# Masked softmax: GpSimd shares ScalarE's fetch of the lengths, fills later, and opens its narrow loads one batch later

## The chip, the cores and the metric

The kernel runs on one core of a Trainium2 chip. The time is the device time of one execution, in microseconds (us). A core has TensorE (PE), VectorE (DVE), ScalarE (ACT), GpSimd (POOL) and SyncE (SP), each with its own queue of instructions; 16 DMA engines move data between main memory and the on-chip memory (SBUF), for all queues together. Engines wait for each other and for transfers by semaphores.

## What is computed

`x` is 16 batches x 8 heads x 256 x 256 in float32, `lengths` has one number from 128 to 255 for each batch. Each row is a softmax over its first `length` columns; the others are zero.

```python
for b in range(batch):
    length = lengths[b]
    masked = x[b, :, :, :length].copy()
    masked = masked - np.max(masked, axis=-1, keepdims=True)
    exp_masked = np.exp(masked)
    result[b, :, :, :length] = exp_masked / np.sum(exp_masked, axis=-1, keepdims=True)
```

## The kernel before

**Tiles.** A batch is 2048 rows of 256 columns: 128 partitions x 16 rows x 256, 2 MB. The tile `xt` has 8 slots of one batch each; batch b lives in slot b mod 8 from its load to its store, and every step works in place. The first four batches (`ahead = 4`) are loaded whole by SyncE's queue. The twelve others are loaded by GpSimd's queue, each only as wide as its length needs (`widths` 160 to 240 in steps of 8, or all 256). Since a narrow load doesn't fill the columns behind it, GpSimd first sets columns 160 to 255 of slots 4 to 7 to zero (L151, "the fills"), and the mask overwrites what is out of range in any case.

**SyncE (L107 to L123)** issues batch 0 in two halves (semaphores `s_ld[0]` and `s_ld[1]`), batches 1 to 3 (`s_ld[2]` to `s_ld[4]`, so batch b has `s_ld[b + 1]`), and then the stores of all batches in order. A store is cut into parts (`parts`, L50): a half and two quarters up to batch 9, two halves for batches 10, 11 and 15, one piece for 12 to 14. It waits for VectorE's divide of that part (`s_out`) and, from batch 2 on, until the store of batch b - 2 has landed. Whole loads and stores go through the same queue, q1 in the profile; GpSimd's loads are q0.

**GpSimd (L142 to L162)** writes the column numbers (`iota_i`) and `ones`, fetches the lengths for itself (`word_p`, L146), seeds the store semaphores, waits for VectorE's first step (`s_v` 1, the column bounds `down`), makes the four fills, and waits for its lengths, the fills, and `s_ld[ahead - 1]`: the landing of batch 2 (L152 to L154). Then a loop issues the narrow loads. It reads the batch's length into a register (L158), and from its third load on waits until the load two before has landed and the store that frees its slot has too (L160, L161); so two narrow loads at most are under way. `pick` (L127) branches to the load of the right width (L131).

**VectorE** makes `down` from `iota_i` (L180), casts the lengths that ScalarE's queue fetched (`word`, L110) to bf16 (L185), and from a TensorE product that spreads them over the partitions (L167) makes `len_s` (L188), the bounds by batch. Both L180 and L188 raise `s_v`. Then for every batch: `mask`, one clip of the batch (L197; batch 0 in halves), and `divide`, twice a reciprocal (L221) and a product of half a batch (L224). The order is written out: batch b + 1 is masked before batch b is divided (L233 to L240), so a batch that lands late holds up the divide, and the store, of the batch before it.

**ScalarE** issues the fetch of `word`, and then for every half batch takes eight exponentials with their row sums (L251), as soon as VectorE has clipped it.

Of the kernel before, what the change touches and what calls it, by code (L numbers as in the profile page):

```python
# [11 lines left out]
I32 = mybir.dt.int32  # L12
# [4 lines left out]
POOL = mybir.EngineType.Pool  # L17
# [3 lines left out]
def kernel(  # L21
# [6 lines left out]
    nc = tc.nc  # L28
    P = nc.NUM_PARTITIONS

    batch, heads, seq_q, seq_k = x.shape
# [10 lines left out]
    ahead = 4  # L42
# [18 lines left out]
    pool = ctx.enter_context(tc.tile_pool(name="all", bufs=1))  # L61
    psum = ctx.enter_context(tc.tile_pool(name="psum", bufs=1, space=bass.MemoryType.PSUM))
    xt = pool.tile([P, slots, nt, seq_k], F32, name="xt")
    word64 = pool.tile([1, batch], mybir.dt.int64, name="word64")
    word = word64.bitcast(I32)
    word64_p = pool.tile([1, batch], mybir.dt.int64, name="word64_p")
    word_p = word64_p.bitcast(I32)
    len_b = pool.tile([1, batch], BF16, name="len_b")
    ones = pool.tile([1, P], BF16, name="ones")
    len_f = psum.tile([P, batch], F32, name="len_f")  # L70
# [8 lines left out]
    with tc.tile_critical(no_gpsimd_drain=True):  # L79
        sem = lambda n: ctx.enter_context(nc.semaphore(n))  # L80
        s_word = sem("s_word")
        s_word_p = sem("s_word_p")
        s_ones = sem("s_ones")
        s_lenb = sem("s_lenb")
        s_lenf = sem("s_lenf")
        s_ld = [sem(f"s_ld{k}") for k in range(ahead + 1)]
# [6 lines left out]
        s_v = sem("s_v")  # L93
# [4 lines left out]
        def length(engine, at):  # L98

            return nc.values_load(  # L100
                at,
                engines=[engine],
                skip_runtime_bounds_check_because="compared with constants, never an address",
            )


        for h in range(2):  # L107
            s = slice(h * half, (h + 1) * half)
            nc.sync.dma_start(out=xt[:, 0, s], in_=x_f[0, :, s]).then_inc(s_ld[h], 16)  # L109
        nc.scalar.dma_start(out=word64, in_=lengths[None, :]).then_inc(s_word, 16)  # L110
        for b in range(1, ahead):
            nc.sync.dma_start(out=xt[:, b], in_=x_f[b]).then_inc(s_ld[b + 1], 16)  # L112
        for b in range(batch):
            s_b = s_st[b % 2]
            for s in parts(b):
                nc.sync.wait_ge(s_out, 2 * b + (s.stop - 1) // half + 1)
                if b >= 2 and s.start == 0:
                    nc.sync.wait_ge(s_b, 64 * (b // 2 + 1))
                nc.sync.dma_start(  # L119
                    out=out_f[b, :, s, :], in_=xt[:, b % slots, s, :]  # L120
# [6 lines left out]
        def pick(v, n, slot, par, ws):  # L127

            if len(ws) == 1:
                w = ws[0]  # L130
                nc.gpsimd.dma_start(  # L131
                    out=xt[:, slot, :, :w], in_=x_n[:, n, :, :w]
                ).then_inc(s_sw[par], 16)
                return
            m = (len(ws) - 1) // 2
            with nc.gpsimd.If(v <= ws[m]):  # L136
                pick(v, n, slot, par, ws[: m + 1])
            with nc.gpsimd.Else():  # L138
                pick(v, n, slot, par, ws[m + 1 :])
# [3 lines left out]
            iota_i, pattern=[[1, seq_k]], base=0, channel_multiplier=0  # L143
        ).then_inc(s_iota, 1)
        nc.gpsimd.memset(ones, 1.0).then_inc(s_ones, 1)  # L145
        nc.gpsimd.dma_start(out=word64_p, in_=lengths[None, :]).then_inc(s_word_p, 16)  # L146
        for par in range(2):
            nc.gpsimd.memset(seed[:, par : par + 1], 0.0).then_inc(s_st[par], 64)  # L148
        nc.gpsimd.wait_ge(s_v, 1)
        for b in range(ahead, slots):  # L150
            nc.gpsimd.memset(xt[:, b, :, low:], 0.0).then_inc(s_fill, 1)  # L151
        nc.gpsimd.wait_ge(s_word_p, 16)  # L152
        nc.gpsimd.wait_ge(s_fill, slots - ahead)
        nc.gpsimd.wait_ge(s_ld[ahead - 1], 16)  # L154
        with nc.Fori(0, (batch - ahead) // 2, 1, engines=[POOL]) as q:  # L155
            for par in range(2):
                n = 2 * q + (ahead + par)
                v_len = length(POOL, word_p[0:1, bass.ds(2 * n, 1)])  # L158
                with nc.gpsimd.If(q >= 1):  # L159
                    nc.gpsimd.wait_ge(s_sw[par], 16 * q)  # L160
                    nc.gpsimd.wait_ge(s_st[par], 64 * q)  # L161
                pick(v_len, bass.ds(n, 1), bass.ds(n % slots, 1), par, widths + [seq_k])  # L162
# [9 lines left out]
        def step(ins):  # L172
# [8 lines left out]
                out=down, in0=iota_i, scalar1=0.5, scalar2=-big, op0=ALU.add, op1=ALU.mult  # L181
# [7 lines left out]
                out=len_s, in0=len_f, scalar1=big, scalar2=None, op0=ALU.mult  # L189
# [56 lines left out]
        with nc.Fori(0, 2 * batch, 1, engines=[ACT]) as i:  # L246
            nc.scalar.wait_ge(s_min, i + 1)
            at = bass.ds(i % (2 * slots), 1)
            for j in range(half):
                e = x_h[:, at, j, :]  # L250
                ins = nc.scalar.activation(  # L251
                    out=e, in_=e, func=EXP, accum_out=sum_h[:, bass.ds(i, 1), j]
# [32 lines left out]
```

The softmax here doesn't subtract the row's maximum and nothing guards it: scores larger than these inputs give would overflow.

## Time and profile before

| | us |
|---|---|
| median of 14 runs (156.74 to 157.53) | 156.96 |
| the profiled execution | 156.46 |
| its span | 154.7 |
| VectorE busy | 120.4 |
| ScalarE busy | 105.1 |
| GpSimd busy | 19.4 |
| batch 0's halves landed | 6.2 and 8.7 |
| batches 1, 2 and 3 landed | 13.6, 18.5 and 24.1 |
| clip of batch 0's first half starts | 9.30 |
| first store issued | 16.73 |
| first narrow load issued | 20.69 |
| last store issued | 143.8 |

Times in the trace count from the span's start. In a row of the timeline the first number is when an instruction started and the second how long it took; what stands in brackets is the engine's idle time before it and what ended it. "Busy" of the DMA engines is the mean share of time in which a packet was under way on the 16 engines; it can be a little over 1 where packets overlap. A landing is the time at which a transfer's semaphore was complete.

### The profile page before, as it was taken

What the parts mean: (1) busy time and instruction counts of PE and PEld (TensorE: products, weight loads), DVE (VectorE), ACT (ScalarE), POOL (GpSimd) and SP (SyncE); (2) the same over time, 40 slices, a digit from 0 to 9 for tenths busy, and PEclk for the clock granted to TensorE, in tenths of its full rate; (3) what the DMA queues carried; (4) which work ended last, traced back from release to release, by engine and by line L of the source; (5) the groups of instructions that cost most, each with busy time, mean ns of one, the idle gap of its engine ahead of it and who ended that gap; (6) DMA issues with size and microseconds to landing.
All of it is one profiled execution on the core that took longest, in us unless ns stands there. A gap on an engine that the chain in (4) does not pass through costs nothing.

```text
span 154.7 us, 1320 instructions
## 1 busy us (share of the span) xinstructions
PE 0.2 (0%) x1; PEld 0.1 (0%) x1; DVE 120.4 (78%) x84; ACT 105.1 (68%) x514; POOL 19.4 (13%) x26
## 2 busy tenths in 40 slices
PE   0000000000000000000000000000000000000000
PEld 0000000000000000000000000000000000000000
DVE  4963999999999994939989499999894999970000
ACT  3019599999989694882959579889796597900000
POOL 7900031003030202002020021120100000000000
DMA  4999999999999999999999999999999999999993
GB/s 117 426 441 428 441 318 380 418 439 434 399 402 396 416 413 410 424 405 410 414 410 421 406 418 408 412 409 409 424 410 450 417 413 424 449 432 441 413 422 140
DMA packets 10452, 62.08 MB, mean 401 GB/s; under 512 B 930, under 2 KB 1026, under 8 KB 7122
## 3 DMA queue, kind: packets, MB, share of 16 engines
q1 hardware_dynamic: 6336, 41.95, 66.3%
q0 software_dynamic: 4112, 20.12, 32.1%
q14 instruction: 2, 0.02, 0.0%
q10 hardware_dynamic: 2, 0.00, 0.0%
HBM read 28.51 MB, written 33.55 MB: 401 GB/s over the span
## 4 chain that ended last, share of the span: by engine, by line
DMA 67%; DVE 15%; issue 3%; SPq 2%; POOLq 1%; DVEq 0%
DMA xt<-in_x_dram 38%; DMA out_dram<-xt 29%; DVE xt L224 10%; DVE xt L197 5%; SPq L119 2%; DVE inv_sum L221 1%; SPq L109 1%; POOLq L100 0%; POOLq L131 0%; POOLq L136 0%; SPq L112 0%; DVEq L214 0%; POOLq L155 0%; POOLq L159 0%; POOLq L138 0%
## 5 line engine op out<-in xcount | busy, mean ns | idle before, releaser
L251 ACT ACTIVATE xt<-xt x256 | 102.4, 401 | 28.6 <-DVE xt L197 28.6
L224 DVE TENSOR_TENSOR xt<-xt,inv_sum 128x2048 f32<-128x2048 f32 x32 | 73.3, 2292 | 1.1
L251 ACT ACTIVATION_READ_ACCUMULATOR xt<-xt x256 | 47.9, 187 | 0.0
L197 DVE SCALAR_TENSOR_TENSOR xt<-down,len_s,xt 128x2048 f32<-128x2048 f32 (+1 forms) x17 | 37.7, 2224 | 12.2 <-DMA xt<-in_x_dram 11.2
L131 POOL DMA_DIRECT2D xt<-in_x_dram x12 | 12.7, 1058 | 90.8 <-DMA out_dram<-xt 51.1
L221 DVE RECIPROCAL inv_sum<-row_sum 128x8 f32<-128x8 f32 x32 | 6.3, 195 | 2.4 <-ACT xt L251 2.4
L185 DVE CAST len_b<-word 1x16 bf16<-1x16 int32 x1 | 5.6, 5602 | 0.4 <-DMA word<-in_lengths_dram 0.4
L151 POOL MEMSET xt<- 128x1536 f32 x4 | 5.3, 1394 | 0.0
L243 ACT ACT_TABLE_LOAD x1 | 1.3, 1283 | 1.6 <-SPq L79 1.6
L180 DVE TENSOR_SCALAR down<-iota_i 128x256 f32<-128x256 int32 x1 | 0.3, 294 | 1.6 <-POOL iota_i L142 1.6
L146 POOL DMA_DIRECT2D word_p<-in_lengths_dram x1 | 0.6, 646 | 0.1
L188 DVE TENSOR_SCALAR len_s<-len_f 128x16 f32<-128x16 f32 x1 | 0.2, 175 | 0.3 <-PE len_f L167 0.3
L142 POOL IOTA iota_i<- 128x256 int32 x1 | 0.3, 332 | 0.6 <-SPq L79 0.6
L243 ACT ACTIVATE warm<-const-float32-0.0 128x1 f32<-128x1 f32 x1 | 0.2, 202 | 0.0
L145 POOL MEMSET ones<- 1x128 bf16 x1 | 0.2, 194 | 0.0
L167 PE MATMUL len_f<-len_b,ones 1*128 1x16 bf16 x1 | 0.2, 164 | 8.1 <-DVE len_b L185 8.1
L269 POOL MEMSET const-float32-0.0<- 128x1 f32 x1 | 0.1, 99 | 0.3 <-issue 0.3
L148 POOL MEMSET seed<- 1x1 f32 x2 | 0.1, 88 | 0.0
L167 PEld LDWEIGHTS len_f<-len_b,ones 1*128 1x128 bf16 x1 | 0.1, 99 | 8.0 <-issue 8.0
L269 POOL MEMSET const-float32-1.0<- 128x1 f32 x1 | 0.1, 99 | 0.0
L269 POOL MEMSET const-bfloat16-1.0<- 128x1 bf16 x1 | 0.1, 99 | 0.0
L269 POOL MEMSET const-uint8-127<- 128x1 uint8 x1 | 0.1, 99 | 0.0
(1 smaller groups left out, 0.0 us busy)
## 6 DMA issues: line engine op xcount, KB each, us to landing
out_dram<-xt SPq DMA_DIRECT2D x16, 1024.0 KB
out_dram<-xt SPq DMA_DIRECT2D x20, 512.0 KB
xt<-in_x_dram SPq DMA_DIRECT2D x3, 2048.0 KB, 16.0
out_dram<-xt SPq DMA_DIRECT2D x3, 2048.0 KB
xt<-in_x_dram POOLq DMA_DIRECT2D x3, 1728.0 KB, 16.3
xt<-in_x_dram POOLq DMA_DIRECT2D x2, 2048.0 KB, 16.5
xt<-in_x_dram POOLq DMA_DIRECT2D x2, 1600.0 KB, 14.0
xt<-in_x_dram POOLq DMA_DIRECT2D x2, 1280.0 KB, 13.9
```

The source lines that it names most:

```text
L109: nc.sync.dma_start(out=xt[:, 0, s], in_=x_f[0, :, s]).then_inc(s_ld[h], 16)
L119: nc.sync.dma_start(out=out_f[b, :, s, :], in_=xt[:, b % slots, s, :]).then_inc(s_b, 16 * ((s.stop - s.start) // quarter))
L131: nc.gpsimd.dma_start(out=xt[:, slot, :, :w], in_=x_n[:, n, :, :w]).then_inc(s_sw[par], 16)
L146: nc.gpsimd.dma_start(out=word64_p, in_=lengths[None, :]).then_inc(s_word_p, 16)
L151: nc.gpsimd.memset(xt[:, b, :, low:], 0.0).then_inc(s_fill, 1)
L185: nc.vector.tensor_copy(out=len_b, in_=word[:, ::2]).then_inc(s_lenb, 1)
L197: return nc.vector.scalar_tensor_tensor(out=t, in0=down[:, None, lo:hi].to_broadcast([P, s.stop - s.start, hi - lo]), scalar=len_s[:, b : ...
L221: step(nc.vector.reciprocal(out=inv_sum[:, b, s], in_=row_sum[:, b, s]))
L224: nc.vector.tensor_tensor(out=t, in0=t, in1=inv_sum[:, b, s, None].to_broadcast([P, half, seq_k]), op=ALU.mult,).then_inc(s_out, 1)
L243: nc.scalar.activation(out=warm, in_=nc.const_aps.tensor(0.0, (P, 1), F32), func=EXP)
L251: ins = nc.scalar.activation(out=e, in_=e, func=EXP, accum_out=sum_h[:, bass.ds(i, 1), j])
L269: nc = _bacc.Bacc("TRN2", target_bir_lowering=False, num_devices=1)
```

## The change

GpSimd no longer fetches the lengths; it reads those that ScalarE's queue fetched (`word`) and waits for that fetch. That fetch's line moves ahead of SyncE's loads in the text; on ScalarE's own queue it was first and stays first. The fills wait for both of VectorE's steps (`down` and `len_s`) instead of the first. The loop of narrow loads waits for the landing of batch 3 (`s_ld[ahead]`), the last whole load, instead of batch 2.

```diff
-    word64_p = pool.tile([1, batch], mybir.dt.int64, name="word64_p")
-    word_p = word64_p.bitcast(I32)
...
+        nc.scalar.dma_start(out=word64, in_=lengths[None, :]).then_inc(s_word, 16)
         for h in range(2):
             s = slice(h * half, (h + 1) * half)
             nc.sync.dma_start(out=xt[:, 0, s], in_=x_f[0, :, s]).then_inc(s_ld[h], 16)
-        nc.scalar.dma_start(out=word64, in_=lengths[None, :]).then_inc(s_word, 16)
...
-        nc.gpsimd.dma_start(out=word64_p, in_=lengths[None, :]).then_inc(s_word_p, 16)
         for par in range(2):
             nc.gpsimd.memset(seed[:, par : par + 1], 0.0).then_inc(s_st[par], 64)
-        nc.gpsimd.wait_ge(s_v, 1)
+        nc.gpsimd.wait_ge(s_v, 2)
         for b in range(ahead, slots):
             nc.gpsimd.memset(xt[:, b, :, low:], 0.0).then_inc(s_fill, 1)
-        nc.gpsimd.wait_ge(s_word_p, 16)
+        nc.gpsimd.wait_ge(s_word, 16)
         nc.gpsimd.wait_ge(s_fill, slots - ahead)
-        nc.gpsimd.wait_ge(s_ld[ahead - 1], 16)
+        nc.gpsimd.wait_ge(s_ld[ahead], 16)
         with nc.Fori(0, (batch - ahead) // 2, 1, engines=[POOL]) as q:
             for par in range(2):
                 n = 2 * q + (ahead + par)
-                v_len = length(POOL, word_p[0:1, bass.ds(2 * n, 1)])
+                v_len = length(POOL, word[0:1, bass.ds(2 * n, 1)])
```

More of the change, by code (lines that the diff above doesn't have):

```diff
@@ L81 @@
         s_word = sem("s_word")
-        s_word_p = sem("s_word_p")
         s_ones = sem("s_ones")
```

## The prediction

> **What bounds the kernel now.** I read the two lines of the DMA engines in the slices first, then the same thing by stages, then the two queues, and only then the engines.
>
> ```profile
> DMA  4999999999999999999999999999999999999993
> GB/s 117 426 441 428 441 318 380 418 439 434 399 402 396 416 413 410 424 405 410 414 410 421 406 418 408 412 409 409 424 410 450 417 413 424 449 432 441 413 422 140
> ...
> q1 hardware_dynamic: 6336, 41.95, 66.3%
> q0 software_dynamic: 4112, 20.12, 32.1%
> ```
>
> Each slice is 3.87 us. The 16 DMA engines are 90% busy or more in all but the first and the last slice, while VectorE is busy for 78% of the span and ScalarE for 68%. Queue q1 carries SyncE's whole loads and all stores, q0 GpSimd's narrow loads. The stages (us, then the busy time of PE, PEld, DVE, ACT and POOL, the clock, the DMA engines' busy share and GB/s):
>
> ```profile
> 0.00:4.00 4.00, 0.00 (x0) 0.00 (x0) 1.99 (x2) 1.49 (x2) 2.87 (x12) 1.00 0.46 127
> 4.00:20.00 16.00, 0.16 (x1) 0.10 (x1) 12.31 (x9) 7.27 (x36) 3.88 (x3) 1.00 1.02 433
> 20.70:23.70 3.00, 0.00 (x0) 0.00 (x0) 3.00 (x3) 3.00 (x17) 1.19 (x1) 1.00 0.91 259
> 25.00:125.00 100.00, 0.00 (x0) 0.00 (x0) 87.99 (x63) 81.84 (x405) 10.95 (x10) 1.00 1.02 414
> 125.00:152.00 27.00, 0.00 (x0) 0.00 (x0) 13.10 (x10) 9.49 (x48) 0.00 (x0) 1.00 1.01 428
> ```
>
> The share stands at 0.91 to 1.02 from 4 us to 152 us. The bytes are fixed by the lengths: 62.08 MB. So the end can move for three reasons only: the transfers start earlier or later, a hole opens in which neither queue has work, or the engines move the same bytes at another rate. One stretch stands out for its rate: from 20.7 to 23.7 us the engines are busy but move 259 GB/s, where the 16 us before it run at 433.
>
> The compute chain at the start, and GpSimd's queue:
>
> ```profile
> 2.30 5.60 DVE L185 CAST len_b<-word 1x16 bf16<-1x16 int32 x1 [0.40 <-DMA word<-in_lengths_dram]
> 2.47 0.12 POOL L148 MEMSET seed<- 1x1 f32 x2
> 2.54 5.34 POOL L151 MEMSET xt<- 128x1536 f32 x4
> ...
> 8.25 0.17 DVE L188 TENSOR_SCALAR len_s<-len_f 128x16 f32<-128x16 f32 x1 [0.35 <-PE len_f L167]
> ...
> 20.69 1.20 POOL L131 DMA_DIRECT2D xt<-in_x_dram  x1 [12.82 <-issue]
> 23.88 0.54 POOL L131 DMA_DIRECT2D xt<-in_x_dram  x1 [1.99 <-issue]
> 36.76 1.17 POOL L131 DMA_DIRECT2D xt<-in_x_dram  x1 [12.34 <-issue]
> ```
>
> A cast of 16 numbers takes 5.60 us and ends at 7.90 us, as the last of the four fills ends at 7.88 us. GpSimd issues its first narrow load at 20.69 us, 2.2 us after the landing that it waits for (18.49 us in the chain of waits).
>
> **Where the times come from.** The profiled execution took 156.46 us: the span of 154.70 and 1.76 around it. The median of the runs is 156.96, so 0.50 above. I sum against 156.46 and add the 0.50 at the end. About 0.2%, 0.3 us, is what a measurement of this kernel can tell from no change.
>
> **Part 1: the fills wait for the bounds (s_v 2 for 1).** The cast starts when the lengths land, at 2.30 us in both. Without fills beside it I give it 0.18 us (len_s, 16 columns, 0.175; the reciprocal, 8 columns, 0.195). From its end to len_s's start passed 0.35 us (7.90 to 8.25), so len_s stands at 2.8 to 3.0 us instead of 8.25. Behind the new wait on GpSimd's queue stand only the fills and the narrow loads; the fills then run from about 3.05 to 8.4 us (5.34 us), and nobody needs them before the narrow loads' gate. The first clip waits no longer for len_s but for the first half of batch 0, which lands at 6.2 us (issue at 1.13, 5.1 to landing); by the 0.23 us from landing to clip seen at 126.05 it starts at 6.4 instead of 9.30, **2.9 us earlier**. The later ones follow: batch 1 lands at 13.6 us, so its clip goes from 16.62 to 13.8; batch 2 lands at 18.5, so 21.32 becomes 18.7; from there VectorE is busy throughout, and the divides and stores of batches 0 to 2 come 2.6 to 2.9 us earlier (first store issued at 13.9 instead of 16.73). What is this worth at the end? Nothing: the stores stand on q1 behind 8.39 MB of whole loads, which at 433 GB/s fill the engines until about 23 us whether a store waits behind them or not. If that cover were gone the gain would be the 2.9 us; the row of 4 to 20 us (share 1.02) says it is whole.
>
> The fills now run beside the first clip (6.4 to 7.7 us). Bounds: nothing, or the clip is held as the cast was, until 8.4 us. Even then it starts 0.7 us earlier than 9.30, and the end doesn't notice. I take nothing; the price is zero by either.
>
> On this the Trainium skill has a rule that can speak against the move ("SBUF — State Buffer", Who interferes with whom): VectorE and GpSimd share a port pair as an exclusive lock, which copies and casts can take in their two-port modes. The 5.60 us cast agrees. By the same section an operation with two SBUF inputs, as the clip is, is held only by a GpSimd operation that reads SBUF, and a fill reads nothing, so by the page the clip runs free; no run here shows that yet. It changes no term.
>
> **Part 2: one fetch of the lengths instead of two.** GpSimd loses one issue of 0.65 us and q0 16 packets. Its own copy was there long before 18.49 us, and ScalarE's lands at 2.3. Nothing at the end. ScalarE's issue stands first on its queue before and after; SyncE's queue is unchanged.
>
> **Part 3: the narrow loads open at batch 3's landing.** Batch 3 lands at 24.14 us (issued at 3.29, longest time to landing 20.9), batch 2 at 18.49: the gate moves by 5.65 us, the first issue from 20.69 to 26.34 and, since q0 moves no data before 26.2 us in this trace (5.5 us after its issue), the first narrow data from 26.2 to 31.9 us. Is there work for the engines from 23 to 31.9? The stores of batches 0 and 1 are issued by 26.4 us (28.96 less 2.6) and are 4.19 MB: at 430 GB/s they last 9.7 us, to 33.0. Batch 2's first half is issued at about 30.7 (33.49 less 2.8), its second at 33.1: 2.1 MB more, to 37.9. **No hole**, with over a microsecond to spare even before batch 2.
>
> Next late is VectorE. Batch 4 now shares the engines with these stores:
>
> ```profile
> q0 software_dynamic: 226, 1.08, 55.3%
> q1 hardware_dynamic: 240, 0.90, 46.2%
> ```
>
> (26.2 to 31 us: packets, MB, share of the stretch). With quarter stores beside it q0 moves 1.08 MB in 4.8 us, 225 GB/s; beside half stores about 145 to 160 (31 to 35 us has 0.75 MB by packets started). Batch 4 is 1.64 MB: 0.72 beside the rest of batch 1 (31.9 to 35), 0.56 beside batch 2's first half (to 38.9), 0.36 at 225: landed at about 40.5 instead of 35.39. VectorE, done with batch 2 at 33.1, stands still for some 7 us where it had not waited at all, and batch 3's first store, which stands behind batch 4's clip (2.35) and a divide (0.2 + 2.3), is issued at about 45.6. Beside the rest of batch 2 (about 0.7 MB) batch 5 has the larger share (79.4% of the engines at 35 to 40 us in this trace, the same pairing) and ends at about 46.4. Batch 6 is issued 1.4 us after batch 4's landing, 41.9, with data 4.6 to 5.5 us later: 46.5 to 47.4. So q0 may stand empty for up to 1 us, with batch 3's store in front of the engines since 45.6. Price: nothing by this count, 1.0 us if q1 has run dry by 45 us. I take nothing, and keep 1.0 as the upper end.
>
> From there the round is as before: a batch costs some 9.4 to 10 us of engine time (issues at 51.71, 61.08, 71.05), VectorE and its 7.2 us fit in. Loads run 4 to 5 us later, stores as much earlier; the last batch lands at about 130.5 instead of 126.05, the last divide ends at 142.8 instead of 138.4, and batch 15's store leaves at 143.41 in any case, when batch 13's has landed. So the tail has room, by about 0.6 us at that store and far more at the engines (batch 14's store still fills them then).
>
> **Part 4: the slow stretch.** 3.0 us at 259 instead of 433 GB/s leave (433 - 259) x 3.0 = 522 KB undone, **1.2 us** of the span. It begins as GpSimd issues its first narrow load and ends with the whole loads. The change takes that issue out of the loads. Bounds: -1.2 us (the issue beside the loads made it), +1.2 (it comes with the issue and again with the loads' end). For the row that it is nearest to I take GpSimd's next narrow issue at 36.76 us: there, beside a load on q0 and stores, the engines move 424 GB/s from 35 to 40 us. So an issue alone makes no such stretch, and I leave it to the change of q1 from loads to stores, which stays: 0.
>
> **Sum:** 0 + 0 + 0 + 0. 156.46 stays, 156.96 on the median; I say **156.9 us**.
>
> **Rivals.**
> - Faster: the slow stretch belongs to narrow descriptors being made while whole loads run, and goes. For it: its start at 20.7, to a tenth of a microsecond that of the issue. Against: 36.76 us. 156.96 - 1.2 = **155.8 us**.
> - Slower: a hole on both queues at about 45 us. Batch 4 comes so late that q1 is empty before batch 3's store, and batch 6's data are not yet there when batch 5 is done. Price 1.0 us, **158.0 us**. It decides if q1 gets more than its 46% beside batch 4, so that batch 2's stores are out before 45 us. Against: the shares above. A slow stretch that comes twice would give 158.2.
> - It doesn't do what it says: the cast is slow by itself, the fills come at 8.4 to 13.8 us, still far ahead of the gate at 24.14, and compute is where it was: 156.9, as forecast, since stores of batches 0 and 1 as they were (the last issued at 28.96) still cover the engines to 33 us.
>
> **Chances.** Forecast with the third rival: 0.43. Faster: 0.33. Slower: 0.24. Leaving out 1 in 10 on either side, the range runs from 155.6 to 158.1; it takes in both rivals and leaves out the stretch made double.
>
> **What would show it.** Right: a cast of about 0.2 us, first clip near 6.4, first store issued near 13.9, first narrow issue near 26.3, batch 4's clip near 40.5 after a wait of some 7 us, DMA share about 1 from 4 to 152 us, and a slow stretch that still ends the whole loads. Wrong: 430 GB/s up to the last whole load (faster), or a slice between 40 and 50 us whose DMA share falls below 0.9 (slower).

## The result, and the profile after

The changed kernel takes 158.01 us (median of 10 runs, 157.72 to 158.26), the kernel before 156.97 beside it (47 runs): ratio **1.0064, 95% interval 1.0052 to 1.0075**. It is slower by 1.0 us. The profiled execution took 157.80 us, with a span of 156.0 (before 156.46 and 154.7).

The slices of the kernel after, 3.9 us each:

```profile
DMA  4999999999999999999999999999999999999992
GB/s 118 422 448 429 437 303 401 424 398 419 441 418 326 386 410 421 409 415 411 404 419 409 419 407 408 411 409 421 401 416 424 447 416 418 452 424 437 418 420 103
```

The line of the busy share is the same 9s as before. Beside the slow slice that was there (303, before 318) the line of GB/s has a second one: 326, the slice from 46.8 to 50.7 us. No slice of before comes near it after the whole loads. The same by stages, kernel after (us, then busy time of PE, PEld, DVE, ACT, POOL, the clock, the DMA share and GB/s):

```profile
20.70:23.70 3.00, 0.00 (x0) 0.00 (x0) 2.93 (x5) 3.00 (x17) 0.00 (x0) 1.00 0.89 262
48.00:51.00 3.00, 0.00 (x0) 0.00 (x0) 3.00 (x2) 3.00 (x16) 1.15 (x1) 1.00 1.03 301
51.00:54.00 3.00, 0.00 (x0) 0.00 (x0) 2.97 (x4) 2.35 (x13) 0.00 (x0) 1.00 1.01 398
```

and of the kernel before, where the new stretch lies:

```profile
48.00:51.00 3.00, 0.00 (x0) 0.00 (x0) 2.50 (x2) 3.00 (x17) 0.00 (x0) 1.00 1.03 404
51.00:54.00 3.00, 0.00 (x0) 0.00 (x0) 2.97 (x3) 1.77 (x10) 1.15 (x1) 1.00 1.04 422
```

At 48 to 51 us the busy share is 1.03 in both, but after the change 301 GB/s pass instead of 404. That is (404 - 301) x 3 = 309 KB left undone, and (422 - 398) x 3 = 72 KB more in the next row: 381 KB, at 414 GB/s **0.92 us** of the 1.05 lost on the median (1.3 in the spans of the two profiled executions). A balance over the whole span agrees: from 48 to 125 us the mean is 409 GB/s against 414, 385 KB, and the stages ahead of it and from 125 to 150 us differ by 72 KB at most.

What moves the data in those 3 us, kernel after (packets, MB, share of the 16 engines' time):

```profile
q0 software_dynamic: 187, 0.88, 101.1%
q1 hardware_dynamic: 6, 0.02, 2.2%
```

It is almost only q0, with batch 6's narrow load. q1 has run dry: by the packet records its packets end at 47.8 us, but for six stragglers of 4 KB, the last of which ends at 49.5. Batch 3's store comes too late, and why stands in the timeline of VectorE and of SyncE's queue, kernel after:

```profile
2.30 0.16 DVE L181 CAST len_b<-word 1x16 bf16<-1x16 int32 x1 [0.40 <-DMA word<-in_lengths_dram]
2.82 0.17 DVE L184 TENSOR_SCALAR len_s<-len_f 128x16 f32<-128x16 f32 x1 [0.35 <-PE len_f L163]
6.51 1.28 DVE L193 SCALAR_TENSOR_TENSOR xt<-down,len_s,xt 128x1024 f32<-128x1024 f32 x1 [3.52 <-DMA xt<-in_x_dram]
...
42.01 2.35 DVE L193 SCALAR_TENSOR_TENSOR xt<-down,len_s,xt 128x2048 f32<-128x2048 f32 x1 [8.89 <-DMA xt<-in_x_dram]
...
44.51 2.29 DVE L220 TENSOR_TENSOR xt<-xt,inv_sum 128x2048 f32<-128x2048 f32 x1
```

```profile
46.83 0.37 SPq L116 DMA_DIRECT2D out_dram<-xt  x1
```

VectorE stands still for 8.89 us until batch 4 lands, clips it, and only then divides batch 3; the store is issued at 46.83. Its first data move at 50.67, 3.84 us later. The start of the kernel, on the other hand, went as planned: the cast takes 0.16 us, and the first clip starts at 6.51.

### The profile page after: what moved, and what is told of

Its sections match the earlier page's. It is cut to its first block, busy times and chain, and to the rows that moved or that the text cites. A ratio compares the mean times of both kernels' runs of the same rounds, so it can differ in the third digit from the quotient of the medians.

```text
span 156.0 us, 1319 instructions
## 1 busy us (share of the span) xinstructions
PE 0.2 (0%) x1; PEld 0.1 (0%) x1; DVE 115.0 (74%) x84; ACT 105.2 (67%) x514; POOL 19.0 (12%) x25
## 3 DMA queue, kind: packets, MB, share of 16 engines
q0 software_dynamic: 4080, 20.12, 32.4%
## 4 chain that ended last, share of the span: by engine, by line
DMA 72%; DVE 12%; issue 3%; SPq 2%; POOLq 2%; DVEq 0%
DMA xt<-in_x_dram 52%; DMA out_dram<-xt 20%; DVE xt L220 9%; DVE xt L193 3%; SPq L116 1%; POOLq L97 1%; SPq L109 1%; SPq L107 1%; DVE inv_sum L217 0%; POOLq L128 0%; POOLq L133 0%; POOLq L155 0%; POOLq L151 0%; DVEq L210 0%; POOLq L135 0%
## 5 line engine op out<-in xcount | busy, mean ns | idle before, releaser
L193 DVE SCALAR_TENSOR_TENSOR xt<-down,len_s,xt 128x2048 f32<-128x2048 f32 (+1 forms) x17 | 37.8, 2224 | 24.4 <-DMA xt<-in_x_dram 24.2
L181 DVE CAST len_b<-word 1x16 bf16<-1x16 int32 x1 | 0.2, 164 | 0.4 <-DMA word<-in_lengths_dram 0.4
```

Source lines behind the costliest of these rows:

```text
L193: return nc.vector.scalar_tensor_tensor(out=t, in0=down[:, None, lo:hi].to_broadcast([P, s.stop - s.start, hi - lo]), scalar=len_s[:, b : ...
```

## Experiments

Two theories. **T1:** the later gate empties q1 at 48 us, and a narrow load without packets of another queue beside it moves fewer bytes while the engines look full. **T2:** the loss comes from elsewhere: from the earlier compute (parts 1 and 2), from the lateness of the narrow loads as such, or from the slow stretch at 21 to 24 us. Each ratio is to the kernel before, in runs on the same chip.

**e1: the gate back at batch 2, the rest of the change kept.**

```diff
-        nc.gpsimd.wait_ge(s_ld[ahead], 16)
+        nc.gpsimd.wait_ge(s_ld[ahead - 1], 16)
```

> The changed kernel with the narrow loads' gate put back to batch 2's landing; the shared fetch and the late fills stay. Theory (the gate alone costs: with it q1 runs dry from 48 to 51 us and a narrow load alone moves only 301 GB/s): 156.9 to 157.0 us, as the kernel before, cast 0.16 us, no stretch between 25 and 125 us under 380 GB/s. Rival (what costs is the fills beside the first clips, or GpSimd reading a tile that VectorE reads too): still about 158.0.

Measured: 157.05 against 156.9, ratio 1.0008 (0.999 to 1.0027). From 48 to 51 us it moves 407 GB/s. So the fetch and the fills cost nothing and gain nothing that these runs could tell, though they bring compute forward by 2.5 us (first store issued at 14.23, before 16.73).

**e2: the kernel before, with only the gate moved to batch 3.**

```diff
-        nc.gpsimd.wait_ge(s_ld[ahead - 1], 16)
+        nc.gpsimd.wait_ge(s_ld[ahead], 16)
```

> The kernel before with the gate alone moved to batch 3's landing. Theory: about 158.0 us, 157.6 at the least, with a stretch of 2 to 3 us near 300 GB/s behind batch 5's landing, when batch 3's store isn't out yet. Since stores of batches 0 to 2 come 2.6 us later here, q1 has a little more left at 45 us, so a smaller loss than the change's is possible. Rival (the gate costs nothing): 157.0.

Measured: 157.65 against 156.9, ratio 1.005 (1.0026 to 1.0074). The gate alone costs. The place expected was wrong, though: 48 to 51 us has 391 GB/s. With compute as late as before, q1 runs dry sooner: it has no packets from 31.4 to 32.2 us, as batch 1's quarter stores, issued at 28.57 us, move no data before 32.22. The stage of e2:

```profile
31.00:33.00 2.00, 0.00 (x0) 0.00 (x0) 2.00 (x1) 2.00 (x11) 0.00 (x0) 1.00 0.97 331
```

(414 - 331) x 2 = 166 KB is 0.4 us of the 0.75 lost; the rest I have not placed. Nor is this stretch T1's: by the packet records most of batch 4's packets of 4.8 KB take 185 ns in it, as they do beside stores (in e3, further down, 229 ns alone), and a few take up to 665. So e2 shows that the gate alone costs, and not that it costs by the mechanism of T1.

**e3: no store before the first four narrow loads have landed** (a single run). It measures q0 by itself.

```diff
+        nc.sync.wait_ge(s_sw[1], 32)
         for b in range(batch):
             s_b = s_st[b % 2]
```

> The changed kernel with SyncE's first store held until batch 7 has landed, so that batches 4 (200 columns), 5 (whole), 6 (168) and 7 (216) are loaded with nothing else on the DMA engines. Theory (a narrow load alone can't fill the engines): some 280 to 310 GB/s for batches 4, 6 and 7, with a busy share of 1, and 430 for batch 5. Rival (the low rate at 48 to 51 us is VectorE, ScalarE or batch 3's waiting store disturbing the load): 400 GB/s or more for all four. Total time well over 160 us in either case. It also shows how long the first store takes from issue to its first data when its queue is empty and narrow loads are under way: 1 us as at the start, or the 3.8 us of the changed kernel.

Measured: 168.96 us, as the first store is issued at 49.75. Stages of e3, in which q0 alone moves data, of batches 4 (200 columns), 5 (whole), 6 (168) and 7 (216):

```profile
29.50:32.50 3.00, 0.00 (x0) 0.00 (x0) 2.97 (x3) 3.00 (x17) 0.00 (x0) 1.00 1.04 358
34.00:37.00 3.00, 0.00 (x0) 0.00 (x0) 2.49 (x3) 1.68 (x9) 1.16 (x1) 1.00 1.03 437
40.00:42.00 2.00, 0.00 (x0) 0.00 (x0) 2.00 (x2) 2.00 (x11) 1.15 (x1) 1.00 1.03 294
44.00:47.00 3.00, 0.00 (x0) 0.00 (x0) 2.93 (x4) 2.78 (x14) 0.00 (x0) 1.00 1.02 382
```

Neither expectation held for all four: the theory's 430 came for batch 5 and its 280 to 310 for batch 6, but not for batches 4 and 7, which are wider; the rival's 400 came for batch 5 alone. At a share of 1.02 to 1.04 the rate goes with the width: 294 for 168 columns, 358 for 200, 382 for 216, 437 for 256, about 1.7 to 1.8 GB/s for each column. In other words a row takes about the same time at each of these widths. Batch 6's queue line for 40 to 42 us in e3,

```profile
q0 software_dynamic: 125, 0.59, 102.8%
```

gives 1.028 x 2 us x 16 / 125 = 263 ns a packet of 7 rows (0.59 MB / 125 = 4.7 KB, 672 bytes a row), 38 ns a row; the other three give 37, 37 and 38. The same batch beside half and quarter stores, kernel before, 42 to 46 us:

```profile
q1 hardware_dynamic: 159, 0.88, 55.9%
q0 software_dynamic: 156, 0.73, 46.6%
```

0.466 x 4 x 16 / 156 = 191 ns a packet, 27 ns a row. And in the kernel after at 48 to 51 us 1.011 x 3 x 16 / 187 = 259 ns. So this is T1's mechanism, measured by itself: alone, a narrow load gains nothing over a whole one; beside a store its short rows do. It goes for the narrow loads' queue only. With q0 empty and q1 alone, with stores, e3 moves 403 GB/s:

```profile
51.00:60.00 9.00, 0.00 (x0) 0.00 (x0) 8.90 (x8) 8.00 (x39) 1.15 (x1) 1.00 1.00 403
60.00:62.00 2.00, 0.00 (x0) 0.00 (x0) 1.97 (x3) 2.00 (x11) 0.00 (x0) 1.00 0.98 328
62.00:64.00 2.00, 0.00 (x0) 0.00 (x0) 1.13 (x1) 2.00 (x11) 0.53 (x1) 1.00 1.10 332
```

The two rows behind it are a slow stretch like that of 21 to 24 us, here with nothing but stores on the engines. The stretch of e3 from 16 to 22.5 us, where there are no stores, has 421 GB/s: no slow stretch at the end of the whole loads.

**e4: no store before batch 3 has landed.**

```diff
+        nc.sync.wait_ge(s_ld[ahead], 16)
         for b in range(batch):
             s_b = s_st[b % 2]
```

> The changed kernel with SyncE's first store held until batch 3 has landed, so that no store stands in the queue behind the last whole load. On the slow stretch of 20 to 23.5 us (281 GB/s): if it comes from stores queued behind loads on the same queue, it goes, 430 GB/s to the end of the loads, which then land 1.0 us earlier, and a pause of 1 to 2 us follows until the first store's data move; if it belongs to the end of the loads themselves, it stays. Time: 158 to 160 us by either.

Measured: 159.51, ratio 1.0172 (1.0142 to 1.0202). The whole loads now run at 430 GB/s to their end, which comes 1 us earlier; then the engines pause from 22.9 to 24.2 us, and a slow stretch comes at 28 to 32 us (336 GB/s) instead. So holding the first stores back moves the stretch and doesn't remove it; in e3, where they are issued at 49.75 us, it came at 60 to 64.

**e5: batch 3 is divided before batch 4 is clipped, gate at batch 3.** It puts stores back on q1 and leaves the narrow loads as late as after the change.

```diff
         for b in range(batch):
...
-            if b + 1 < batch:
+            if b + 1 < batch and b != ahead - 1:
                 mask(b + 1, slice(0, nt))
             if b > 0:
                 divide(b, 0)
             divide(b, 1)
+            if b == ahead - 1:
+                mask(b + 1, slice(0, nt))
```

> The changed kernel, gate at batch 3's landing kept, but VectorE divides batch 3 before it masks batch 4, so that batch 3's 2 MB of stores are issued by about 38 us instead of 46.8 to 49.7 and q1 has work while batch 6 is loaded. Theory (the loss is q1 running dry because batch 3's divide stood behind batch 4's clip, and a narrow load alone moves 300 GB/s): the stretch of 48 to 51 us moves 400 GB/s or more, and the time goes back to 157.0, 157.3 at most. Rival (the loss is that loads come later, whatever q1 holds): 157.7 to 158.0.

Measured: 157.51 against 157.09, ratio 1.0025 (1.0007 to 1.0044); the interval lies wholly below that of the change. The time is below the rival's 157.7 and above the 157.3 that the theory gave at most. Stages, and the queues from 48 to 51 us, of e5:

```profile
48.00:51.00 3.00, 0.00 (x0) 0.00 (x0) 2.97 (x3) 3.00 (x17) 1.15 (x1) 1.00 1.01 410
51.00:54.00 3.00, 0.00 (x0) 0.00 (x0) 2.97 (x3) 3.00 (x16) 0.00 (x0) 1.00 1.01 386
```

```profile
q1 hardware_dynamic: 106, 0.75, 61.7%
q0 software_dynamic: 101, 0.48, 39.3%
```

Batch 3's stores are issued from 37.83 us, q1 has packets at 48 us, and the stretch is gone, with batch 6's data as late as after the change (47.43 against 47.10). (1.0064 - 1.0025) / 0.0064 = 61% of the loss is back, 31 to 89% by the interval of e5. The rest, about 0.4 us, is not explained. The row of 51 to 54 us at 386 is no part of it: by the bytes moved e5's profiled execution is ahead of that of before at 49 us, level with it from 55 to 118, and about 0.1 MB (0.2 us) behind at 151.

**e6: the gate at batch 1. e8: e5's order with the gate at batch 2.** Edits: `s_ld[ahead - 2]` in the gate; and e5 with `s_ld[ahead - 1]`.

> The changed kernel with the gate at batch 1's landing (13.6 us), one batch earlier than the kernel before. Narrow data then come from about 21 us, beside batch 3's whole load. Theory: both queues hold work throughout, as in the kernel before, so 156.9, 0.3 us to either side; a gate is worth nothing as long as no queue runs dry. Rival (each batch of earlier opening is worth 0.5 to 1 us): 156.2. It also shows whether the slow stretch of 20 to 23.5 us stays when narrow data run beside the last whole load.

> Batch 3 divided before batch 4 is masked, with the gate at batch 2's landing. Theory: q1 isn't dry there in any case (batch 4's clip waited for nothing), so nothing is gained: 156.9 to 157.1. Rival (more stores in hand is worth something at any time): 156.5.

Measured: 0.9996 (0.9976 to 1.0016) and 1.0 (0.9979 to 1.0021). With the gate at batches 1, 2 and 3 the ratios are 0.9996, 1.0008 and 1.0064: flat, then a step. Loads that come later cost nothing as such, until q1 runs dry; and e5's order is worth nothing where it doesn't.

**e9: the gate waits for batch 0's store too.** It makes the narrow loads still later.

```diff
         nc.gpsimd.wait_ge(s_ld[ahead], 16)
+        nc.gpsimd.wait_ge(s_st[0], 128)
```

> The changed kernel with the gate later still: batch 3 landed and batch 0's store landed (about 28.6 us), 4.2 us after the change's. Theory: stores of batches 0 to 2 keep the engines full to about 38 us; then batch 4 (200 columns) is loaded nearly alone at the 342 GB/s of the held-store run for 4 to 5 us, 0.8 us lost, batch 5 (whole) alone at 428 with nothing lost, and batch 3's store is there for batch 6. So about as much is lost as in the change, not in proportion to the lateness: 157.7 to 158.3. Rival (what counts is how late the loads are: 5.7 us of gate cost 1.05 us, so 9.9 us cost 1.8): 158.8.

Measured: 159.71, ratio 1.018 (1.0152 to 1.0207), above what either theory gave. The first narrow load is issued at 32.19, batch 3's store at 49.42, and the store's first data move at 52.70; q1 has had no packets since 46.0. The stage of e9 in which batch 6 is alone until 52.7:

```profile
48.00:54.00 6.00, 0.00 (x0) 0.00 (x0) 5.97 (x4) 5.70 (x30) 1.15 (x1) 1.00 0.95 295
```

Against 413 GB/s (the mean of 404 and 422 before) this leaves (413 - 295) x 6 = 708 KB, 1.7 us (by the share of 0.95 a part of it is idle engines); the whole loss is 2.8. The miss was in the count of how long q1 stays dry: I had not seen that batch 6's data come sooner, 1.9 us after the issue, with q1 idle, and so have the engines to themselves for longer. From 36 to 38 us, where batch 4 is nearly alone, the rate is 365, but not by slow rows: most of its packets take 185 ns, as beside stores, and a few up to 868.

**e7 and e12: e1 with batches 1 to 3 loaded by ScalarE's queue (one kernel, run on two chips). e11: the same with the gate at batch 1.** Is the slow stretch made by stores behind loads on one queue?

```diff
         for b in range(1, ahead):
-            nc.sync.dma_start(out=xt[:, b], in_=x_f[b]).then_inc(s_ld[b + 1], 16)
+            nc.scalar.dma_start(out=xt[:, b], in_=x_f[b]).then_inc(s_ld[b + 1], 16)
```

> The changed kernel with the gate at batch 2's landing and batches 1 to 3 loaded through ScalarE's queue instead of SyncE's, so that no store ever stands behind a whole load on one queue. If the slow stretch of 20 to 23.5 us comes from that, it goes, and the time falls by up to 1 us to 156.0; stores of batch 0 then share the engines with batches 2 and 3, which land later, and a dry q1 later on could take some of it back. If the stretch belongs to the first mixing of loads and stores on the engines, it moves to where the first store's data run, and the time stays near 157.0.

> Whole loads 1 to 3 on ScalarE's queue and the gate at batch 1's landing. Theory: what counts is that q1 and q0 both hold work whenever a narrow load is under way; an earlier gate gives more of that, so the time is that of the same kernel with the gate at batch 2's landing or a little less, 156.2 to 156.6. Rival: batch 4's narrow load takes the engines from batches 2 and 3, which land later, VectorE stands still and q1 runs dry at 25 to 35 us: 157.0 or more.

> The kernel with batches 1 to 3 on ScalarE's queue and the gate at batch 2's landing once more, beside the kernel before, since its gain of 0.25% lies near what can be told: 156.5, ratio under 1, if the gain is real; 156.9 if it was chance.

Measured: 156.54, ratio 0.9975 (0.9958 to 0.9992), and again 156.71, ratio 0.9979 (0.9965 to 0.9994); e11 156.5, ratio 0.9971 (0.9954 to 0.9987). These beat the kernel before by 0.2 to 0.3%, and so the changed one too. Stage of e7:

```profile
20.00:23.00 3.00, 0.00 (x0) 0.00 (x0) 3.00 (x2) 2.90 (x15) 1.29 (x1) 1.00 0.95 300
```

So the stretch stays, with loads and stores on queues of their own, though the time is below the 157.0 expected for that case. Whether it is milder there is not shown: from 20 to 24 us e7 and e12 move 328 GB/s and e11 354, but with all of them on SyncE's queue one execution moves 270 (e1), another 299 (before), 309 (e5) or 327 (e6, with the gate at batch 1 as in e11). What e7 gains over e1 stays open.

**e10: e7 with the stores of batches 0 to 9 in halves.**

```diff
-            cuts = [0, half, half + quarter, nt]
+            cuts = [0, half, nt]
```

> Whole loads 1 to 3 on ScalarE's queue, the gate at batch 2's landing, and the stores of batches 0 to 9 in two halves instead of a half and two quarters. If what the engines need for their packets bounds the kernel: 2560 packets of 4096 bytes at 159 ns become 1280 of 8192 at 309, which takes (2560 x 159 - 1280 x 309) / 16 = 0.7 us off each engine, from 156.5 to 155.8. Rival: the larger packets only shift the share between the queues, and loads come later: 156.5 or more.

Measured: 159.43, ratio 1.016 (1.0132 to 1.0187), 3.6 us above the 155.8 expected; the rival, that loads come later, holds. By the packet records a narrow load has some 39% of the engines beside half stores, and in e7 some 55% beside quarters. So loads come later: q0's last packet ends at 136.8 us, in the kernel before at 125.5. q1 runs dry at 82 us, and near the end both queues do. Stages of e10:

```profile
82.00:85.40 3.40, 0.00 (x0) 0.00 (x0) 2.54 (x2) 3.40 (x18) 0.00 (x0) 1.00 1.02 351
...
143.60:145.60 2.00, 0.00 (x0) 0.00 (x0) 1.97 (x3) 2.00 (x11) 0.00 (x0) 1.00 0.00 0
```

So the small packets of the quarters kept the loads up with the stores. The 2.5 us lost against the kernel before lie at the end: from 142 to 146 us e10 moves 119 GB/s and the kernel before 438, (438 - 119) x 4 = 1276 KB, 3.0 us at 430 GB/s. From 82 to 86 us (361 against 412) e10 only gives back a lead that it had, 400 against 398 GB/s up to there.

## Why the prediction was wrong, step by step

- **Part 1, worth nothing at the end: right.** Cast 0.16 us (forecast 0.18), len_s at 2.82 (2.8 to 3.0), first clip 6.51 (6.4), first store issued 13.95 (13.9). e1 shows that the earlier start is worth nothing at the end. The open bound, a clip held by the fills, went the free way: 1.28 us with the fills (3.05 to 8.4 us) beside it and 1.28 for the second half at 8.95 without. That is as the Trainium skill has it ("SBUF — State Buffer", Who interferes with whom), and the cast's fall from 5.60 to 0.16 agrees as well.
- **Part 2, one fetch instead of two, worth nothing: right**, in e1 too. Only its count was off: q0 has 4080 packets instead of 4112, so 32 fewer and not 16.
- **Part 4, the slow stretch stays: right**, 262 GB/s against 259. GpSimd's issue has moved to 27.25 us and the stretch has not, which ends the faster rival. Its cause as I put it, q1's change from loads to stores, does not hold: e7 has it with loads and stores on two queues, e4 has it some 4 us behind that change, and e3 has one with stores alone.
- **Part 3, "No hole" and "I take nothing": the step that failed.** Its times were near: first narrow issue 27.25 (forecast 26.34; batch 3 landed at 24.39 instead of 24.14, and the read of the length took 1.11 us in the chain, 0.51 before), first narrow data 32.35 (31.9), batch 4's clip 42.01 after 8.89 us (40.5 after 7), batch 3's first store issued 46.83 (45.6), batch 6's data 47.10 (46.5 to 47.4). Two things in it were wrong. First, **"with batch 3's store in front of the engines since 45.6"**: a store is in front of the engines when its data move, and with a narrow load under way that was 3.84 us after the issue. e3's first store, with no narrow load under way, took 0.84; by that the data would have come at 47.7, just as q1's other packets end, at 47.8. (That q1's own stragglers held them up until 49.5 doesn't account for it: in e9, with q1 empty for 3.4 us before the issue, the wait was 3.28.) Second, I priced only a time in which **both** queues are empty and took a share of 1 as full. An empty q1 beside a narrow load is enough: 301 GB/s at 1.03. This was the price of 0.92 us that the sum had at nothing.
- **The slower rival, 158.0:** its time was met and half of its mechanism. q1 did run dry because batch 4 came late. But q0 was never empty (batch 5's last packets end at 47.27, batch 6's first start at 47.10), nothing stood still, and its deciding point, q1 dry before 45 us, was not reached. The upper end that I kept for Part 3, 1.0 us, was the price; that a hole on both queues had been priced at the same is luck.
- **The third rival** fell with the cast of 0.16 us.
- **The tail: right in its order, late by what Part 3 lost.** The last batch lands at 131.67 (forecast 130.5), the last divide ends at 144.00 (142.8), and the last two stores are issued 1.3 us later than before, as the transfers ahead of them are. The prediction had them at the time of before "in any case", which held only without that loss.
- **The sign named, "a slice between 40 and 50 us whose DMA share falls below 0.9", was the wrong instrument:** no share fell, the GB/s did. The prediction had used just that distinction for 20.7 to 23.7 us, and not for the new stretch.

So T1 holds for the loss of this change: the gate alone costs (e2), the rest does not (e1), a narrow load alone is slow (e3), and q1 refilled gives most of the loss back at unchanged lateness (e5). What stays open: the 0.4 us that e5 does not give back; how e2 loses its 0.75 us, as the rows in its dry stretch were not slow; why a store's first data take 3.3 to 3.8 us with a narrow load under way; and what makes the slow stretch.

## What to carry to other kernels

When two queues share the DMA engines, ask of every moment which of them has packets, and read GB/s beside the busy share: full engines can move a quarter less. Before a load is delayed, follow it to the store that is computed behind it in program order, and count that store from its first data, not from its issue. A gate has a flat side and a step; here the step is where the other queue runs dry.

## What the runs showed of the hardware that was not expected

- A narrow load with the engines to itself takes 37 to 38 ns a row at 672 to 1024 bytes (294 to 437 GB/s, e3); 672-byte rows beside half and quarter stores take 27 ns, with 404 GB/s in all (before). Stores alone moved 403 (e3). It doesn't hold from the first packet: at the start of batch 4, with hardly a store beside it, e2 and e9 have most 800-byte rows at 31 ns, as beside stores.
- From a store's issue to its first data: 0.84 us with no narrow load under way (e3), 3.28 with one under way and q1 empty since 46.0 (e9), 3.84 in the kernel after, where q1 still had packets of its own for a part of it. From a narrow load's issue to its first data, with nothing of its own queue ahead: 2.03 us with idle engines (batch 4 in e3), 5.10 beside stores (batch 4 in the kernel after).
- The parts into which stores are cut set the loads' share: some 55% beside quarters in e7, 39% beside halves in e10, which differs from e7 in that alone and took 2.9 us longer.
- In the slow stretch single packets take up to twice as long: those of 16 KB 1137 ns at the median from 21 to 22 us in the kernel before, where 611 is the rule; those of 8 KB 588 from 63 to 64 us in e3, where 316 is. The cause is open.
